# Cross-covariance attention on one core: the last unit's Q and K in 4 KB rows, the last V transfer and the last store in one piece

## The chip, the core and the metric

The kernel runs on one core of a Trainium2 chip. The metric is the device time of one execution in microseconds (us), the median of three runs: 128.64 us before the change (128.51 to 128.71). The core has a matrix engine (PE; its weight loads are listed as PEld), a vector engine (DVE), a scalar engine (ACT), a general engine (POOL) and a sync engine (SP). In this kernel SP issues almost all transfers between the chip's memory (HBM) and the on-chip memory; sixteen DMA engines carry them out.

## What is computed

Q, K and V are float32 of shape (8, 12, 512, 64): 96 heads of 512 rows by 64 columns. Attention is taken over the 64 columns, not over the 512 rows:

```
Q_norm = Q / (norm(Q, axis=-2) + 1e-10)
K_norm = K / (norm(K, axis=-2) + 1e-10)
attn = softmax(einsum('bhnd,bhne->bhde', Q_norm, K_norm), axis=-1)
out = einsum('bhnd,bhde->bhne', V, attn)
```

Each input is 12.58 MB and so is the output, so that 50.33 MB have to pass between HBM and the core.

## The kernel before

**Units.** Four heads are a unit (`HU`); there are U = 24 units, S = 12 pairs of units (unit u is half r of pair s, u = 2s + r) and W = 6 groups of four units. The last unit is u = 23, that is pair 11, half 1.

**Q and K.** `load_qk` (line 172) brings a unit of Q or of K into 128 partitions. For an ordinary unit each head fills 32 partitions with 16 rows of 64 numbers each, so that a partition receives one contiguous run of 4 KB from HBM. `WIDE` (line 118) is the first unit that is loaded differently: there a head fills 64 partitions with 8 rows each, in two halves `m`, and a partition receives two runs of 2 KB (line 183, the views `Qw` and `Kw` of lines 132 and 133). With `WIDE = U - 1` this is the last unit alone. Pairs 0 to 2 and the last pair are loaded one unit at a time, the others as whole pairs (`parts`, line 377).

**Grams.** `cast_qk` (line 209, DVE) puts Q and K of a unit side by side in bf16, and `grams` (line 221) multiplies this block by itself on PE. One product of a head gives all of Q'Q, Q'K and K'K, 128 by 128, accumulated over the steps t. An ordinary unit takes 16 steps of 4 heads, 64 matmuls over 32 partitions; the unit in 2 KB rows takes 8 steps of 4 heads, 32 matmuls over 64 partitions. Every matmul also has a weight load. From the grams the norms (`squares`, `sums`, `powers`), the scaled logits (`scale_k`, `logits`), the exponentials (`exps`) and the normalised weights `ab` (`normalise`) are made.

**V and the output.** `load_v` (line 189) brings two units' V as 128 partitions with one run of 8 KB each, a transfer of 1 MB; the last one, (w, r) = (5, 1), is brought in two halves of 4 KB runs (line 418, line 196). `cast_v` makes bf16 of it in two parts c, `vtrans` transposes on PE, `vcopy` brings the result from PSUM, `outs` multiplies by the weights, `ocopy` copies a quarter of a pair's result to the tile `so`, and `store` (line 198) writes half a pair, 512 KB, in runs of 2 KB. There are 24 such halves, i = 0 and 1 of each pair. Two are special. Store (9, 1), named `FEW` (line 122), goes out as four DMAs: 92 partitions, 4 partitions and 32 partitions of its first half, then the second half (lines 201 to 206). The last store, (11, 1), goes out as two DMAs of 256 KB in runs of 1 KB, each as soon as its own quarter is copied (lines 457 and 458).

**What sets the order.** Nothing is scheduled by the hardware: the class `Order` (line 22) simulates the engines with the costs that are written beside each piece, always takes the piece that can begin first (ties by a rank), and the program emits the pieces in that order. For DMA it assumes at most eight transfers under way (`QUEUE`, line 32), which mirrors the program: its DMAs take eight completion semaphores in turn, and a DMA is issued when the eighth before it has landed. Loads and stores are all on SP, in order. The plan also knows that PE stops now and then for more instructions: `pause` (line 44) counts PE instructions (a matmul and its weight load are two) and expects a stop at 190 and at every 256 after that, until 6.1 us after the previous one. `size` (line 353) tells it how many PE instructions a piece has: 128 for the grams of a unit, 64 for those of a unit from `WIDE` on, 16 for a transposition, 8 for half of one and for the logits, 16 for a quarter of the output.

Of the kernel before, what the change touches and what calls it, by code (L numbers as in the profile page):

```python
# [16 lines left out]
J = T // 2  # L17
# [85 lines left out]
def kernel(  # L103
# [7 lines left out]
    nc = tc.nc  # L111
    B, H, N, _ = Q.shape
    assert N == 32 * T and Q.shape[3] == D
    U = B * H // HU
    S = U // 2
    W = S // 2
    TAIL = 2
    WIDE = U - 1
    ONE = 3
    HELD, UNTIL = ("lk", 1, 1), ("cq", 0, 1)  # L120
    BOTH = S - 8
# [40 lines left out]
    qk32, v32, vb, qkb, gram, scr, kq, n2, r8, kqs, rq, lg, ex, ab, vps, vt, po, so = ({} for _ in range(18))  # L162
# [9 lines left out]
    def load_qk(s, x, r):  # L172
# [7 lines left out]
        if (s, x) == (0, 1):  # L180
            nc.scalar.dma_start(out=qk32[s][:, x, r].rearrange("p t d -> p (t d)"), in_=Ku[w, e, :, r])
        elif 2 * s + (r or 0) >= WIDE:
            nc.sync.dma_start(out=qk32[s][:, x, r].rearrange("p (m j) d -> p m (j d)", m=2), in_=(Qw, Kw)[x][U - 1])
# [11 lines left out]
        else:  # L195
            nc.sync.dma_start(out=o[:, c], in_=i[:, c])

    def store(s, i, k=None):
        rows = slice(None) if k is None else slice(k * (J // 2), (k + 1) * (J // 2))
        o = Of[s // 2, s % 2, i].rearrange("p r (j d) -> p r j d", d=D)  # L200
        if (s, i) == FEW:

            for a, b in ((0, 92), (92, 96), (96, 128)):
                nc.sync.dma_start(out=o[a:b, 0], in_=so[s, i][a:b, 0])
            nc.sync.dma_start(out=o[:, 1], in_=so[s, i][:, 1])
            return
        nc.sync.dma_start(out=o[:, :, rows], in_=so[s, i][:, :, rows])

    def cast_qk(u, x):
        s, r = divmod(u, 2)  # L210
# [10 lines left out]
    def grams(u):  # L221
# [3 lines left out]
        if r == 0:  # L225
            gram[s] = ps_g.tile([128, HU, 2, 2, 2 * D], F32, name="gram")
        for t in range(T if u < WIDE else J):
            for h in range(HU):
                if u < WIDE:
                    x = qkb[u][32 * h:32 * (h + 1), t, :]  # L230
                else:
                    x = qkb[u][64 * (h % 2):64 * (h % 2 + 1), J * (h // 2) + t, :]
                nc.tensor.matmul(gram[s][:, h, r, 0], x, x, start=(t == 0), stop=(t == (T if u < WIDE else J) - 1))  # L233

# [118 lines left out]
    def size(key):  # L353
        if key[0] == "gr" and key[1] >= WIDE:
            return 64
        return 8 if key[0] == "vt" and key[-1] is not None else {"gr": 128, "lg": 8, "vt": 16, "ou": 16}[key[0]]

    plan = Order(size)
    X = 1.29
    R = dict(cq=2.5, gr=2.471, sq=0.756, kq=1, rd=3.457, pw=3.5, sc=1, rq=1.9, lg=5, ex=1.1, nm=2.545, cv=1.165, vt=0.9, vc=1.1, ou=2, oc=0.9)  # L360
    BIAS = dict(sc=-0.6, kq=5, cv=1, vc=-0.3, oc=0.6)
    QK_PACE, V_FROM, V_PACE, ST_LAG = 0.631, 0.0377, 0.7486, 1.5133

    def v_at(v):
        return V_FROM + V_PACE * v / U

    def piece(key, engines, after, behind, rank, fn, *args):
        if key[0] in ("cv", "vc", "oc", "kq", "sc"):
            plan.add(key, engines, after, behind, rank, lambda eng: fn(eng, *args))
        else:  # L370
            plan.add(key, engines, after, behind, rank, lambda eng: fn(*args))

    def back(kind, i, n, *rest):
        return (kind, i - n, *rest) if i - n >= 0 else None
# [17 lines left out]
    for u in range(U):  # L392
        s, r = divmod(u, 2)
# [17 lines left out]
    def turns(w):  # L411
        return [(q, f) for q in range(4) for f in ((0, 1) if w == W - 1 and q >= TAIL else (None,))]

    last, turned = None, None
    for w in range(W):
        both = 2 * w >= BOTH
        for r in range(2):
            halves = (0, 1) if (w, r) == (W - 1, 1) else (None,)
            n = 2 * w + r - NB["v"]
            for c in halves:  # L420
                free = [("cv", n // 2, n % 2, h) for h in range(2)] if n >= 0 else []
                piece(("lv", w, r, c), {"DMA": X if c is not None else 2 * X}, free, [last], v_at(4 * w + 2 * r + (c or 0)), load_v, w, r, c)
                last = ("lv", w, r, c)
            for c in range(2):
                free = [("vt", w - NB["vb"], *t) for t in turns(w - NB["vb"])] if w >= NB["vb"] else []
                piece(("cv", w, r, c), {"POOL": 1.15, "DVE": (0.72, BIAS["cv"])} if both else {"POOL": 1.15},
                      [("lv", w, r, c if len(halves) == 2 else None)] + free, [("cv", w, r, 0)] if c else [], R["cv"] + 0.01 * (4 * w + 2 * r + c), cast_v, w, r, c)
        for n, (q, f) in enumerate(turns(w)):
            if f is None:
                before = turns(w)[n - 1] if n else turns(w - 1)[-1] if w else None  # L430
                wait = [("vc", w if n else w - 1, *before)] if before else []
            else:
                wait = [("kq", S - 1)] + ([("vc", w, *turns(w)[n - 4])] if n >= 4 and turns(w)[n - 4][1] is not None else [])
            piece(("vt", w, q, f), {"PE": 0.6 if f is not None else 0.8}, [("cv", w, r, c) for r in range(2) for c in range(2)] + wait, [turned],
                  R["vt"] + 0.02 * w, vtrans, w, q, f)
            turned = ("vt", w, q, f)
            copies = {"ACT": 0.74 if f is not None else 1.31}
            if both:
                copies["DVE"] = (0.74 if f is not None else 1.42, BIAS["vc"])
            free = [("ou", 2 * (w - NB["vt"]) + e, x) for e in range(2) for x in range(4)] if w >= NB["vt"] else []  # L440
            piece(("vc", w, q, f), copies, [("vt", w, q, f)] + free, [("vc", w, *turns(w)[n - 1])] if n else [], R["vc"] + 0.02 * w, vcopy, w, q, f)
    for s in range(S):
        for x in range(4):
            i, k = divmod(x, 2)
            n = 4 * s + x - 2
            wait = [("oc", n // 4, n % 4)] if n >= 0 else []
            order = [("ou", s, x - 1) if x else back("ou", s, 1, 3)]
            piece(("ou", s, x), {"PE": 0.5}, [("vc", s // 2, *t) for t in turns(s // 2) if t[0] // 2 == k] + [("nm", s)] + wait, order, R["ou"] + 0.01 * s, outs, s, x)
            n = 2 * s + i - NB["so"]
            free = [("st", n // 2, n % 2)] if k == 0 and n >= 0 else []  # L450
            order = [("oc", s, x - 1) if x else back("oc", s, 1, 3)]
            piece(("oc", s, x), {"ACT": 0.6, "DVE": (0.68, BIAS["oc"])} if s >= BOTH else {"ACT": 0.6}, [("ou", s, x)] + free, order, R["oc"] + 0.01 * s, ocopy, s, x)
        for i in range(2):
            order = [("st", s, 0) if i else back("st", s, 1, 1)]
            if (s, i) == (S - 1, 1):

                piece(("sh", s, i), {"DMA": 0.67}, [("oc", s, 2)], order, v_at(2 * s + i) + ST_LAG, store, s, i, 0)
                piece(("st", s, i), {"DMA": 0.67}, [("oc", s, 3)], [("sh", s, i)], v_at(2 * s + i) + ST_LAG, store, s, i, 1)
            else:
                piece(("st", s, i), {"DMA": X}, [("oc", s, 2 * i), ("oc", s, 2 * i + 1)], order, v_at(2 * s + i) + ST_LAG, store, s, i)  # L460

    ahead = [loaded(x, 0, r) for r in range(2) for x in range(2)]
    held, passed = [], False
# [40 lines left out]
```

## Time and profile before

| what | value |
|---|---|
| time, median of 3 runs (lowest, highest) | 128.64 us (128.51, 128.71) |
| the profiled execution: span from first to last instruction | 127.0 us |
| what lies around the span: median less span | 1.64 us |
| instructions in the profile | 4887 |
| PE matmul busy, weight loads busy | 77.7 us (61%), 62.9 us (50%) |
| DVE, ACT, POOL busy | 92.8 us (73%), 72.5 us (57%), 36.6 us (29%) |
| moved by DMA | 50.64 MB in 15629 packets, mean 399 GB/s |

The page gives the profiled execution's span but no device time of its own, so the span stands for it; the 1.64 us around it are taken as constant. The page divides the span into 40 slices of 3.2 us and shows for each the share of time that an engine was busy, in tenths, and what the DMA engines moved. Further down it lists the DMA queues, a chain of work traced back from the end, groups of like instructions with the mean duration of one, and the issues of DMAs. The trace itself can be asked for the instructions in order of time, for the busy time of each engine in a chosen stretch with the number of instructions in it, and for who waited for whom. It also holds, for each DMA, one completion event from each DMA engine that took part, and for each packet its start, duration and size.

### The profile page before, as it was taken

How to read it: one execution, taken by the hardware profiler on the slowest of the kernel's cores; microseconds unless marked ns; L12 is line 12 of the kernel's file. 1: busy time of each engine (PE TensorE's matmuls, PEld its weight loads, DVE VectorE, ACT ScalarE, POOL GpSimd, SP SyncE). 2: the span in 40 equal slices, each digit the busy share in tenths (PEclk: the TensorE clock that was granted, in tenths of full speed). 3: DMA queues.
4: the chain of work that ended last, by engine and by line, in shares of the span. 5: the costliest groups of instructions: out<-in, count | busy, mean ns of one | idle time of the engine just before them, and what ended most of it. 6: DMA issues, size and time to landing. Idle time of an engine off the chain costs nothing.

```text
span 127.0 us, 4887 instructions
## 1 busy us (share of the span) xinstructions
PE 77.7 (61%) x2128; PEld 62.9 (50%) x2128; DVE 92.8 (73%) x141; ACT 72.5 (57%) x220; POOL 36.6 (29%) x40
## 2 busy tenths in 40 slices
PE   0065384894844679858594879566797869680000
PEld 0054372773633568647482668445585748460000
DVE  3354749859899899999885898999999799820000
ACT  4000441569877077786692786794829969972000
POOL 4006307300906903033065212213453361200000
PEclk9999999999998555999958967998559995955555
DMA  4999999999999999999999999999999999999993
GB/s 114 415 434 410 430 410 418 417 437 403 425 426 415 410 419 421 405 415 426 430 410 413 415 421 427 412 419 428 401 413 410 403 402 406 401 405 408 405 366 106
DMA packets 15629, 50.64 MB, mean 399 GB/s; under 512 B 1144, under 2 KB 1656, under 8 KB 14200
## 3 DMA queue, kind: packets, MB, share of 16 engines
q1 hardware_dynamic: 15320, 49.29, 96.4%
q10 hardware_dynamic: 288, 1.05, 2.1%
q8 instruction: 16, 0.26, 0.7%
q14 instruction: 5, 0.04, 0.1%
HBM read 37.75 MB, written 12.58 MB: 396 GB/s over the span
## 4 chain that ended last, share of the span: by engine, by line
DVE 39%; DMA 21%; PE 13%; ACT 11%; issue 4%; POOL 2%; DVEq 0%; SPq 0%; POOLq 0%; ACTq 0%
DMA qk<-in_Q_dram 21%; DVE qkb L213 15%; PE gram L233 9%; DVE scr L240 7%; DVE ab L291 6%; ACT vt L166 4%; DVE vb L168 4%; ACT ex L282 3%; ACT so L166 3%; PE vps L302 3%; DVE n L252 2%; DVE vt L168 2%; DVE so L168 2%; PE po L319 1%; ACT kq L166 1%
## 5 line engine op out<-in xcount | busy, mean ns | idle before, releaser
L233 PE MATMUL gram<-qkb 32*128 32x128 bf16 (+1 forms) x1504 | 35.5, 257 | 23.1 <-DVE qkb L213 9.9
L233 PEld LDWEIGHTS <-qkb 32*128 32x128 bf16 (+1 forms) x1504 | 29.9, 114 | 27.7 <-DVE qkb L213 12.7
L213 DVE CAST qkb<-qk 128x1024 bf16<-128x1024 f32 x48 | 36.4, 780 | 8.5 <-DMA qk<-in_Q_dram 6.9
L170 POOL TENSOR_SCALAR vb<-v 128x1024 bf16<-128x1024 f32 x19 | 21.2, 1129 | 45.5 <-DMA v<-in_V_dram 32.0
L166 ACT COPY so<-po 128x512 f32<-128x512 f32 x45 | 25.0, 593 | 5.2 <-PE po L319 5.0
L166 ACT COPY vt<-vps 128x1024 bf16<-128x1024 bf16 (+1 forms) x18 | 17.8, 989 | 17.4 <-PE vps L302 17.3
L302 PE MATMUL vps<-identb,vb 128*128 128x128 bf16 x192 | 20.2, 262 | 5.8 <-POOL vb L170 3.7
L319 PE MATMUL po<-ab,vt 128*64 128x128 bf16 x384 | 19.3, 242 | 5.2 <-issue 2.7
L263 POOL TENSOR_TENSOR kqs<-kq,r 64x512 f32<-64x512 f32 x12 | 14.0, 1164 | 25.8 <-ACT r L259 13.4
L240 DVE SCALAR_TENSOR_TENSOR scr<-gram,eye 64x512 f32<-64x512 f32 x24 | 16.5, 687 | 4.4 <-PE gram L233 4.1
L302 PEld LDWEIGHTS <-vb 128*128 128x128 bf16 x192 | 14.7, 117 | 10.0 <-POOL vb L170 5.1
L319 PEld LDWEIGHTS <-vt 128*64 128x64 bf16 x384 | 13.8, 121 | 9.2 <-issue 4.6
L282 ACT ACTIVATE ex<-lg,rq 128x64 f32<-128x64 f32 x48 | 14.5, 322 | 2.8 <-PE lg L276 2.7
L166 ACT COPY kq<-gram 64x512 f32<-64x512 f32 x12 | 7.0, 581 | 13.5 <-DVE scr L240 13.4
L291 DVE TENSOR_TENSOR ab<-ex,rinv 64x256 bf16<-64x256 f32 x24 | 13.9, 579 | 0.6
L282 ACT ACTIVATION_READ_ACCUMULATOR ex<-lg,rq 128x1 f32 x48 | 10.2, 213 | 0.0
L168 DVE CAST vb<-v 128x1024 bf16<-128x1024 f32 x5 | 7.6, 1527 | 1.2 <-DMA v<-in_V_dram 1.2
L252 DVE TENSOR_REDUCE n<-scr 128x8 f32<-128x512 f32 x12 | 8.1, 679 | 0.1
L276 PE MATMUL lg<-eye,kqs 64*128 64x64 f32 x48 | 6.4, 259 | 2.6 <-issue 1.5
L168 DVE COPY vt<-vps 128x1024 bf16<-128x1024 bf16 (+1 forms) x8 | 7.9, 1019 | 0.1
L276 PEld LDWEIGHTS lg<-eye,kqs 64*128 64x128 f32 x48 | 4.5, 156 | 4.4 <-issue 2.0
L288 DVE RECIPROCAL rinv<-esum 128x4 f32<-128x4 f32 x12 | 2.1, 171 | 2.8 <-ACT ex L282 2.8
(17 smaller groups left out, 16.0 us busy)
## 6 DMA issues: line engine op xcount, KB each, us to landing
v<-in_V_dram SPq DMA_DIRECT2D x11, 1024.0 KB, 17.1
out_dram<-so SPq DMA_DIRECT2D x22, 512.0 KB, 10.2
qk<-in_Q_dram SPq DMA_DIRECT2D x8, 1024.0 KB, 17.4
qk<-in_K_dram SPq DMA_DIRECT2D x8, 1024.0 KB, 17.1
qk<-in_Q_dram SPq DMA_DIRECT2D x8, 512.0 KB, 12.2
qk<-in_K_dram SPq DMA_DIRECT2D x6, 512.0 KB, 12.5
qk<-in_K_dram ACTq DMA_DIRECT2D x2, 512.0 KB, 7.3
v<-in_V_dram SPq DMA_DIRECT2D x2, 512.0 KB
```

The source lines that it names most:

```text
L166: nc.scalar.copy(o, i)
L168: nc.vector.tensor_copy(o, i)
L170: nc.gpsimd.tensor_scalar(out=o, in0=i, scalar1=1.0, scalar2=0.0, op0=ALU.mult, op1=ALU.add)
L213: nc.vector.tensor_copy(qkb[u][:, :, x * D:(x + 1) * D], qk32[s][:, x, r])
L233: nc.tensor.matmul(gram[s][:, h, r, 0], x, x, start=(t == 0), stop=(t == (T if u < WIDE else J) - 1))
L240: nc.vector.scalar_tensor_tensor(out=scr[s][half], in0=gram[s][half, :, :, 0, half].rearrange("p h r d -> p (h r) d"), scalar=1e-20, in1=e ...
L263: (nc.vector if eng == "DVE" else nc.gpsimd).tensor_tensor(out=kqs[s][HI], in0=kq[s][HI], in1=r8[s][HI, :, None].to_broadcast([D, 2 * HU, ...
L276: nc.tensor.transpose(l[:, h, :], kqs[s][HI, 2 * h:2 * h + 2].rearrange("p r d -> p (r d)"), eye2[HI])
L282: nc.scalar.activation(e[:, h, :], lg[s][:, h, :], AF.Exp, scale=rq[s][:, h:h + 1], accum_out=z[:, h:h + 1])
L291: nc.vector.tensor_tensor(out=a[half, :, half], in0=e[half], in1=ri[half, :, None].to_broadcast([D, HU, D]), op=ALU.mult,)
L302: nc.tensor.transpose(ps[:, c, n, :], vb[w][:, J * c + j].rearrange("p r d -> p (r d)"), identb)
L319: nc.tensor.matmul(po[s, x][e * D:(e + 1) * D, j].rearrange("p r d -> p (r d)"), v, ab[s][:, h, :])
```

## The change

The constant `WIDE` becomes U, so that no unit is loaded in 2 KB rows: the last unit's Q and K come in runs of 4 KB, and its grams take 64 matmuls over 32 partitions in place of 32 over 64. They are still one transfer each for Q and K of that unit, of 512 KB. The last V transfer comes as one of 1 MB in runs of 8 KB. The last store is one of 512 KB in runs of 2 KB, and waits for both of its quarters. `size` now says 128 for the last unit's grams, and the plan is computed anew.

```diff
-    WIDE = U - 1
+    WIDE = U
...
-    def store(s, i, k=None):
-        rows = slice(None) if k is None else slice(k * (J // 2), (k + 1) * (J // 2))
+    def store(s, i):
...
-        nc.sync.dma_start(out=o[:, :, rows], in_=so[s, i][:, :, rows])
+        nc.sync.dma_start(out=o, in_=so[s, i])
...
-            halves = (0, 1) if (w, r) == (W - 1, 1) else (None,)
+            halves = (None,)
...
-            if (s, i) == (S - 1, 1):
-
-                piece(("sh", s, i), {"DMA": 0.67}, [("oc", s, 2)], order, v_at(2 * s + i) + ST_LAG, store, s, i, 0)
-                piece(("st", s, i), {"DMA": 0.67}, [("oc", s, 3)], [("sh", s, i)], v_at(2 * s + i) + ST_LAG, store, s, i, 1)
-            else:
-                piece(("st", s, i), {"DMA": X}, [("oc", s, 2 * i), ("oc", s, 2 * i + 1)], order, v_at(2 * s + i) + ST_LAG, store, s, i)
+            piece(("st", s, i), {"DMA": X}, [("oc", s, 2 * i), ("oc", s, 2 * i + 1)], order, v_at(2 * s + i) + ST_LAG, store, s, i)
```

## The prediction

> **What bounds the kernel.** I read the 40 slices first, then the DMA queues, then stretches of the end. The transfers run from the start to the end, and they outlive the computing:
>
> ```profile
> span 127.0 us, 4887 instructions
> ...
> PE   0065384894844679858594879566797869680000
> ...
> DMA  4999999999999999999999999999999999999993
> GB/s 114 415 434 410 430 410 418 417 437 403 425 426 415 410 419 421 405 415 426 430 410 413 415 421 427 412 419 428 401 413 410 403 402 406 401 405 408 405 366 106
> ...
> q1 hardware_dynamic: 15320, 49.29, 96.4%
> ...
> q8 instruction: 16, 0.26, 0.7%
> ```
>
> The DMA row has a 9 in every slice but the first and the last, PE has zeros in the last four. So the end is that of the sixteen DMA engines, and an engine's work sets it, not a wait of the computing. Keep the q8 row in mind: 16 packets of 16 KB each, which carry instructions and not data. The last copy to `so` ends at 115.07 us; SP issues stores up to 120 us:
>
> ```profile
> 114.00 1.07 ACT L166 COPY so<-po 128x512 f32<-128x512 f32 x2 [0.24 <-PE po L319]
> ...
> 115.75 4.76 SPq L207 DMA_DIRECT2D out_dram<-so  x5
> ```
>
> The five issues (the single records: 115.75, 117.05, 118.30, 119.58, 120.05) wait for a free place among the eight DMAs under way, not for data. In the stretches of the end (last two columns: DMA share, GB/s) the rate falls before it stops:
>
> ```profile
> 120.00:122.00 2.00, 0.00 (x0) 0.00 (x0) 0.00 (x0) 0.00 (x0) 0.00 (x0) 0.50 1.06 407
> 122.00:123.00 1.00, 0.00 (x0) 0.00 (x0) 0.00 (x0) 0.00 (x0) 0.00 (x0) 0.50 0.92 353
> 124.00:125.00 1.00, 0.00 (x0) 0.00 (x0) 0.00 (x0) 0.00 (x0) 0.00 (x0) 0.50 0.73 258
> 125.00:126.00 1.00, 0.00 (x0) 0.00 (x0) 0.00 (x0) 0.00 (x0) 0.00 (x0) 0.50 0.08 26
> ```
>
> The engines don't end together. The last DMA's sixteen completion events stand at 122.48, 122.69, 123.03, 124.00, 124.81, 125.07, 125.13, then eight from 125.25 to 125.54, and one alone at 126.05, which ends the execution. The store before `FEW` shows why: eight engines complete it at 116.44 to 118.09, eight at 119.11 to 119.52. Tracing the events back, each 16 KB packet makes one engine later by 1.0 to 1.5 us: the first eight packets hit eight different engines, the ninth (66.03 us) makes one of these doubly late, and by the sixteenth (108.57 us) all eight have had two. `FEW`'s 92 rows go to four of the other eight engines; one of these is now the last, 0.51 us behind the eight.
>
> **Part 1: fewer, larger packets.** In each size most packets start on their engine a fixed time after the one before: 42.3 ns at 1 KB, 80 at 2 KB, 155.4 at 4 KB, 306 at 8 KB. Per engine: Q and K of the last unit 2 x (16 x 80 - 8 x 155.4) = 74 ns; last V 16 x 155.4 - 8 x 306 = 38 ns; last store 32 x 42.3 - 16 x 80 = 74 ns; two completion packets fewer, about 10 ns. Together 0.19 us on every engine, the last one too. By the packets' own durations (46, 84, 159, 309 ns, and 9 for a completion) it is 0.36 us. I take 0.19, since starts fix the rate, and keep 0.10 and 0.36 as ends.
>
> The Trainium skill ("DMA: Bandwidth & Descriptors", "Anatomy of one DMA" and "Rules for kernel authors") gives a DMA a fixed 2.0 us and tells authors to coalesce; by that, two DMAs fewer would be worth 4 us, and the sum would be about 124.6. That formula is given for the path through the general engine; here the two halves of the last store complete 0.68 us apart on the last engine (125.37 and 126.05), half of a whole store's 1.28, so nearly all of such a cost lies under the queue.
>
> **Part 2: 64 more PE instructions.** The grams of unit 23 go from the second of these forms to the first, from 32 pairs of matmul and weight load to 64:
>
> ```profile
> L233 PE MATMUL gram<-qkb 32*128 32x128 bf16 x1472 | 34.4, 257 | 23.1 <-DVE qkb L213 9.9 <-DVE qk L179 6.7 <-issue 4.8
> ...
> L233 PE MATMUL gram<-qkb 64*128 64x128 bf16 x32 | 1.1, 217 | 0.0
> ```
>
> Their own time is cheap: 1.07 us now, 1.89 for 64 in the chain of work. What counts is the number. PE stops at intervals with nothing in the profile to wait for ("issue"):
>
> ```profile
> 62.22 0.13 PEld L276 LDWEIGHTS lg<-eye,kqs 64*128 64x128 f32 x1 [1.59 <-issue]
> ...
> 68.42 0.50 PEld L233 LDWEIGHTS <-qkb 32*128 32x128 bf16 x33 [1.59 <-issue]
> ```
>
> Cut at these stops, the number of PE and PEld instructions (x, first two pairs of columns) is:
>
> ```profile
> 0.00:62.21 62.21, 37.03 (x1119) 30.47 (x1119) 48.15 (x74) 32.65 (x96) 20.05 (x25) 0.92 0.99 404
> 62.21:68.41 6.20, 4.87 (x128) 3.95 (x128) 4.44 (x8) 4.16 (x16) 2.36 (x3) 0.72 1.00 415
> 68.41:80.80 12.39, 9.56 (x256) 7.61 (x256) 11.01 (x17) 8.52 (x22) 3.40 (x3) 0.86 1.02 417
> 86.72:104.76 18.04, 14.88 (x384) 11.80 (x384) 16.82 (x25) 13.11 (x38) 7.43 (x7) 0.81 1.03 407
> 104.76:127.00 22.24, 7.91 (x113) 6.26 (x113) 6.53 (x13) 9.45 (x32) 1.04 (x1) 0.58 0.93 356
> ```
>
> 2238 = 190 + 8 x 256, then 256, 512, and (after one of 256 not shown) 768: pages of 256 instructions, each crossing followed 3 to 6 us later by one 16 KB packet. PE resumes at 62.22, 1.3 us after the end (60.88) of the packet that the crossing before had called for, so a crossing fetches the page that begins at the next one. The last crossing is number 4030; 226 instructions follow, to 4256. The next would be 4286. With 64 more there are 4320, so it is crossed, 34 instructions before the end, and a **seventeenth packet** is due some 4 us later, near 120 us, while the engines still drain stores.
>
> Its price: it hits an engine that has had two, presumably the first of the lap, whose events have stood at the late end of the eight since (125.53). The last two packets, which fell among stores as this one will, made their engines about 1.1 us later; the packet alone lasts 0.94; the early ones, among loads, cost up to 1.5. I take 1.1. The end: 125.53 - 0.19 + 1.1 = 126.44, against 126.05 now: **+0.39 us**. From the first of the eight, 125.25, at 0.94 and a saving of 0.36 it is below the engine that is last today, and that one's saving decides; from 125.54 at 1.5 and a saving of 0.10 it is +0.89.
>
> The Trainium skill ("Runtime: NRT & Kernel Launch", "Instruction fetch mechanics") also has 256-instruction blocks of 16 KiB and calls a crossing "mostly hidden"; by that the seventeenth is free and only part 1 remains. For PE that doesn't hold in the rows above (1.59 us each), and it says nothing of the data engine that carries the packet.
>
> **Part 3: what becomes late in the computing.** Up to the grams of unit 23 PE has run 3904 instructions (1952 pairs before 99.96 us). With 128 they reach 4032, so the last pair lies beyond crossing 4030 and waits for its page. That page's packet ended at 103.37 and PE resumed at 104.77; the grams now end at 101.04. The squares of pair 11 start at 102.94 today (DVE is busy until then) and would start near 105.0, +2.1 us. V as a whole lands near 101.5, so its first cast starts 1.1 us later than at 100.36; the transpositions behind it stand behind the PE stop anyway. The last copy then ends near 117.2, or 118 if the clock, 0.5 to 1.0 in this stage, falls less well. Behind it wait the last store on SP and nothing else. SP has no place for that store before 119.58, so up to there nothing changes. Beyond that the late engines still write the store before it (completed at 123.88 to 124.20 on the eight), and a store reaches the engines about 1 us after its issue (119.58, first 1 KB packet 120.5); they lack nothing before an issue at about 122. The cover is some 5 us; were it gone, each us later would be a us.
>
> Losing the early half of the last store (part 1's other side) costs nothing either: both halves are issued after 115.07, when both have data.
>
> **Rivals.**
> *No seventeenth packet reaches the drain* (fetching ends with the program, or an early engine takes it). For: the page from 4286, which the sixteenth brought, may hold the program's last instructions; then it was needed and a further one isn't. Against: only a handful of PE instructions shows after 4256, and the sixteenth was fetched all the same. Then 126.05 - 0.19: **128.45 us**, 128.28 to 128.54: not slower.
> *The computing reaches the drain.* Decides from a last copy past 122 us, 7 us later than now; at 124 it gives 2 us more, about 130.6. Against: I count 2 to 3.
> *Fixed costs were not hidden, or the merged transfers balance the engines anew*: up to 1 us less, about 127.7. Against: other transfers in the same forms already run back to back.
>
> **The numbers.** Sums are in the profiled execution (span 127.0) and are added to the median, 128.64, 1.64 above it. The likeliest case, 0.70, gives 128.64 + 0.39 = 129.03, own range 128.45 to 129.53. No packet 0.22, computing 0.05, balance 0.03. A measurement of this kernel can tell about 0.2%, 0.26 us. Of the likeliest case 0.72 lies above that (0.50), 0.26 within (0.18), the rest below (0.02); of the second 0.35 is faster (0.08), else the same (0.14); the third is slower, the fourth faster. Faster 0.13, same 0.32, slower 0.55. Leaving out the second case would leave out too much, so the range is 128.4 to 129.5.
>
> **What would show it.** Right: q8 with 17 packets; the last PE stretch 34 instructions after a stop at 4286; a stop of about 3 us before the last pair of unit 23's grams; one late-group engine completing the last store alone, near 126.4; no packets of 1 KB. Wrong: q8 with 16; the last event again from the engine of `FEW`; copies that end past 120 us, with SP waiting for ACT at its last issue.

## The result, and the profile after

| | before | after |
|---|---|---|
| time, median (lowest, highest) | 128.57 us (128.51, 128.71) | 129.28 us (129.21, 129.49) |
| ratio, 95% interval | | 1.0049 (1.0034 to 1.0065) |
| span of the profiled execution | 127.0 us | 127.4 us |
| instructions in the profile | 4887 | 4949 |
| last completion event of the last store | 126.05 us | 126.53 us |

The changed kernel is slower by 0.6 us, 0.4 to 0.8 by the interval. The forecast was 0.39 us more, in a range that holds the measured time.

From the profile of the changed kernel, the rows that were shown of before (slices of the span, then the DMA queues: packets, MB, share of 16 engines):

```profile
span 127.4 us, 4949 instructions
...
PE   0065393994837679859475986777597729753000
...
DMA  4999999999999999999999999999999999999991
GB/s 113 413 438 408 428 411 418 417 433 408 435 418 414 411 417 424 402 415 427 423 414 414 415 428 417 415 424 425 401 420 419 401 402 410 395 408 408 375 377 60
...
q1 hardware_dynamic: 14648, 49.29, 95.9%
...
q8 instruction: 17, 0.28, 0.8%
```

The same 49.29 MB now go in 672 packets fewer on q1, and q8 has 17 packets in place of 16. PE still has its zeros at the end, but three of them in place of four. The crossing at 4030 (a crossing is the place where one block of 256 PE instructions, a page, ends and the next begins) fell into the last unit's grams, as forecast. First the weight loads of PE in order of time, then the instructions on either side of the stop (x of PE and of PEld):

```profile
99.96 0.90 PEld L232 LDWEIGHTS <-qkb 32*128 32x128 bf16 x63
104.47 0.09 PEld L232 LDWEIGHTS <-qkb 32*128 32x128 bf16 x1 [3.61 <-issue]
```

```profile
0.00:104.46 104.46, 67.98 (x2015) 55.78 (x2015) 84.43 (x127) 61.45 (x186) 36.01 (x38) 0.89 1.01 408
104.46:127.40 22.94, 9.01 (x145) 6.96 (x145) 8.48 (x16) 10.89 (x34) 1.04 (x1) 0.75 0.91 350
```

63 of the 64 pairs run, the last waits 3.61 us; 2 x 2015 = 4030 is the crossing, to the instruction. 290 instructions follow in place of 226, so that the next crossing, 4286, is passed 34 before the last. In the trace's packets the seventeenth of 16 KB starts at 117.65 us and lasts 0.96 us. What it does is seen in two places. SP in order of time:

```profile
111.44 1.93 SPq L203 DMA_DIRECT2D out_dram<-so  x3
114.30 0.37 SPq L204 DMA_DIRECT2D out_dram<-so  x1
115.63 5.50 SPq L206 DMA_DIRECT2D out_dram<-so  x4
```

The single records of the last row are 115.63, 116.91, 119.72 and 120.75: a gap of 2.8 us where 1.3 is usual, since the store eight places before was complete on fifteen engines at 118.14 and on the sixteenth at 119.65. And the end, in stretches (last two columns: DMA share, GB/s):

```profile
120.00:122.00 2.00, 0.00 (x0) 0.00 (x0) 0.00 (x0) 0.00 (x0) 0.00 (x0) 0.50 0.99 384
122.00:123.00 1.00, 0.00 (x0) 0.00 (x0) 0.00 (x0) 0.00 (x0) 0.00 (x0) 0.50 1.05 406
124.00:125.00 1.00, 0.00 (x0) 0.00 (x0) 0.00 (x0) 0.00 (x0) 0.00 (x0) 0.50 0.59 227
125.00:126.00 1.00, 0.00 (x0) 0.00 (x0) 0.00 (x0) 0.00 (x0) 0.00 (x0) 0.50 0.07 29
126.00:127.00 1.00, 0.00 (x0) 0.00 (x0) 0.00 (x0) 0.00 (x0) 0.00 (x0) 0.50 0.01 4
```

Before, the stretch from 126 on moved nothing (0 GB/s). A share of 0.07 of sixteen engines is one engine: it writes alone for about the last microsecond. The completion events of the last DMA, one from each engine, say the same:

```
before  122.48 122.69 123.03 124.00 124.81 125.07 125.13 125.25 125.28 125.31 125.34 125.37 125.41 125.53 125.54 126.05
after   123.55 123.57 123.68 124.34 124.37 124.75 125.11 125.12 125.13 125.21 125.22 125.24 125.34 125.36 125.50 126.53
```

Fifteen engines are done by 125.50 (before, by 125.54, and the sixteenth 0.5 us later). Now the sixteenth is one of the late group and is 1.0 us behind. The trace doesn't name the engine of an event; but the same lag can be followed from store to store back to the one of 118.14 and 119.65, where it sets in while the seventeenth packet is under way, so that this engine is taken to be the one that carried the packet.

### The profile page after: what moved, and what is told of

Read it like the earlier page. It is cut to its first block, busy times and chain, and to the rows that moved or that the text cites. A ratio compares the mean times of both kernels' runs of the same rounds, so it can differ in the third digit from the quotient of the medians.

```text
span 127.4 us, 4949 instructions
## 1 busy us (share of the span) xinstructions
PE 77.0 (60%) x2160; PEld 62.7 (49%) x2160; DVE 92.9 (73%) x142; ACT 72.3 (57%) x220; POOL 37.0 (29%) x39
## 3 DMA queue, kind: packets, MB, share of 16 engines
q1 hardware_dynamic: 14648, 49.29, 95.9%
## 4 chain that ended last, share of the span: by engine, by line
DVE 36%; PE 21%; DMA 19%; issue 8%; ACT 5%; SPq 1%; DVEq 0%; ACTq 0%
DVE qkb L212 15%; DMA qk<-in_K_dram 14%; PE gram L232 12%; DVE scr L239 7%; DMA qk<-in_Q_dram 5%; DVE vt L168 4%; PE vps L301 4%; DVE ab L290 4%; PE po L318 3%; ACT so L166 3%; DVE n L251 2%; ACT ex L281 2%; DVE vb L168 2%; PE lg L275 1%; SPq L185 1%
## 5 line engine op out<-in xcount | busy, mean ns | idle before, releaser
L232 PE MATMUL gram<-qkb 32*128 32x128 bf16 x1536 | 36.7, 259 | 24.8 <-issue 8.5
L232 PEld LDWEIGHTS <-qkb 32*128 32x128 bf16 x1536 | 30.8, 116 | 29.7 <-issue 11.1
L212 DVE CAST qkb<-qk 128x1024 bf16<-128x1024 f32 x48 | 37.7, 810 | 9.6 <-DMA qk<-in_Q_dram 8.0
L170 POOL TENSOR_SCALAR vb<-v 128x1024 bf16<-128x1024 f32 x18 | 21.7, 1215 | 43.9 <-DMA v<-in_V_dram 39.0
L301 PE MATMUL vps<-identb,vb 128*128 128x128 bf16 x192 | 18.5, 253 | 4.8 <-POOL vb L170 3.5
L301 PEld LDWEIGHTS <-vb 128*128 128x128 bf16 x192 | 14.0, 113 | 7.9 <-POOL vb L170 4.2
L290 DVE TENSOR_TENSOR ab<-ex,rinv 64x256 bf16<-64x256 f32 x24 | 12.8, 534 | 0.6
```

The lines of the kernel that those rows point to most:

```text
L170: nc.gpsimd.tensor_scalar(out=o, in0=i, scalar1=1.0, scalar2=0.0, op0=ALU.mult, op1=ALU.add)
L212: nc.vector.tensor_copy(qkb[u][:, :, x * D:(x + 1) * D], qk32[s][:, x, r])
L290: nc.vector.tensor_tensor(out=a[half, :, half], in0=e[half], in1=ri[half, :, None].to_broadcast([D, HU, D]), op=ALU.mult,)
L301: nc.tensor.transpose(ps[:, c, n, :], vb[w][:, J * c + j].rearrange("p r d -> p (r d)"), identb)
```

## The experiments

Three theories were held against each other. **The page:** 64 PE instructions more, past one more crossing, bring a seventeenth packet, and it makes one DMA engine the last. **The merging:** the whole V, the whole last store or the 4 KB rows fill the engines worse or come late. **The computing:** the longer grams and their stop delay the last stores. The kernel before, run beside the experiments, had 128.65 to 128.66 us; ratios are against it.

**1. Rows and grams put back**, V and store stay whole:

```diff
-    WIDE = U
+    WIDE = U - 1
```

> The changed kernel with 2 KB rows and 64-row grams put back for the last unit; V transfer and last store stay whole. Theory of the page (the seventeenth packet of PE instructions makes one twice-hit DMA engine the last): 4256 PE instructions, 16 packets, and only the saving of the merged V and store is left, 0.04 + 0.07 + 0.01 = 0.12 us: 0.1 to 0.2 us under the kernel before, about 128.45. Rival of the merging (the whole V or the whole last store is late or fills the engines worse): the loss stays, 129.0 to 129.3. Rival of the computing (longer grams and their stop delay the stores): as the theory, since the grams are short again; it is told apart by the runs with added matmuls.

128.44 us, 0.9983 (0.9975 to 0.9992), 16 packets. The loss is gone, and the merged V and store bring 0.2 us: faster than both kernels.

**2. Rows and grams alone**, the kernel before with `WIDE = U`:

> The kernel before with only the last unit's rows and grams changed (WIDE = U); V and the last store stay in halves. Theory of the page: 17 packets, the whole loss and without the 0.12 us that the merging saves: 0.1 us above the changed kernel, about 129.4 (0.8 above before). Rival of the merging: no loss, 128.5 to 128.6. Rival of the computing: as the theory, with a last copy after 115.1 us and SP waiting for ACT near the end.

129.22 us, 1.0055 (1.0042 to 1.0067), 17 packets. The whole loss is there with V and the store in halves. That it would be 0.1 us above the changed kernel doesn't show; the intervals don't separate them. With the first run this rules out a merged V or store as the cause, but the 4 KB rows and the grams still go together.

**3 to 6. Matmuls alone.** The kernel before, all its transfers as they were, with n pairs of matmul and weight load ahead of the last unit's grams, whose results the real ones overwrite; n = 14 and 16, then 8 and 24:

```diff
+        for n in range(14 if u == U - 1 else 0):
+            x = qkb[u][64 * (n % 2):64 * (n % 2 + 1), n % T, :]
+            nc.tensor.matmul(gram[s][:, n % HU, r, 0], x, x, start=True, stop=True)
         for t in range(T if u < WIDE else J):
```

> The kernel before with 14 more pairs of matmul and weight load in the last unit's grams, overwritten by the real ones; all transfers as before. 4284 PE instructions, 2 short of the crossing at 4286. Theory of the page: 16 packets, time of the kernel before within 0.1 us, 128.6. Rival of the computing: grows with the matmuls, some 0.3 us of the 0.7 (28 of the 64 instructions). Rival of the merging: no change.

> As the run with 14, but 16 more pairs: 4288 PE instructions, 2 past the crossing at 4286. Theory of the page: 17 packets and a step of the whole loss, plus 0.6 to 0.9 us over the kernel before, 129.2 to 129.5, though only four instructions more than the run with 14 pairs. Rival of the computing: within 0.05 us of the run with 14 pairs. Rival of the merging: no change against before.

These two missed: 129.15 us, 1.0040 (1.0021 to 1.0060), and 129.25 us, 1.0034 (1.0014 to 1.0055), no step between them, and both spread over more than 1.4 us (128.49 to 129.93, 128.44 to 129.86). The spans tell more. With 14 pairs all twelve are 126.7 to 127.1, as before; the time around the span (time less span of one execution), 1.74 to 1.85 in the executions of the kernel before, is 1.76 to 2.83. With 16 pairs two spans are long, 127.8 and 128.1 (the profiled one is the first, and has 17 packets), the other ten are 126.6 to 127.0 with 1.74 to 3.05 around them. So within a few instructions of the crossing it isn't the same in every execution whether the span grows, and something costs time outside the span; the traces don't show what. I had put the runs too near. The next two stand clear of it:

> The kernel before with 8 more pairs (4272 PE instructions, 14 short of the crossing at 4286), farther from it than the run with 14. Theory of the page: 16 packets in every execution, 128.66 within 0.1 us, and the time around the span at its usual 1.78 us, unlike the 1.8 to 2.8 of the run with 14 pairs. Rival of the computing: a little above before. If the spread of the run with 14 comes of the added matmuls and not of the nearness of the crossing, half of it shows here.

> The kernel before with 24 more pairs (4304 PE instructions, 18 past the crossing), farther past it than the run with 16. All transfers as before. Theory of the page: 17 packets in every execution, the spans at 127.5 to 128.1 as in the three executions of the run with 16 that had them, time 129.2 to 129.6, narrow. Rival of the computing: no more than 0.2 us over before. Rival of the merging: as before.

(The run with 16 had two such spans, not three, from 127.8 on.) With 8 pairs 128.64 us, 0.9996 (0.9987 to 1.0005): nothing. With 24 pairs 129.78 us, **1.0083 (1.0069 to 1.0097)**, all five between 129.40 and 129.93. Sixteen pairs lie between the two, at most 0.5 us of PE's time (64 take 1.89 us), and 1.1 us of the kernel's. PE doesn't stop at the crossing at 4286 in the profile (0.05 us between the instructions on either side), and the last copy ends at 116.92 us, where that of the faster seventh run, below, ends at 116.89. The queue of instructions, and the last stretches, of the run with 24 pairs:

```profile
q8 instruction: 17, 0.28, 0.8%
```

```profile
124.00:125.00 1.00, 0.00 (x0) 0.00 (x0) 0.00 (x0) 0.00 (x0) 0.00 (x0) 0.50 0.73 258
125.00:126.00 1.00, 0.00 (x0) 0.00 (x0) 0.00 (x0) 0.00 (x0) 0.00 (x0) 0.50 0.18 64
126.00:127.00 1.00, 0.00 (x0) 0.00 (x0) 0.00 (x0) 0.00 (x0) 0.00 (x0) 0.50 0.05 16
```

From 124 to 125 it moves what the kernel before moved there, 258 GB/s; then it goes on for 1 us longer, at last on one engine alone, with its event at 127.05 us, where the other fifteen are done by 126.00.

**7. All the transfers of the change, without the added instructions:**

```diff
-        for t in range(T if u < WIDE else J):
+        for t in range(J if u == U - 1 else T):
...
-                nc.tensor.matmul(gram[s][:, h, r, 0], x, x, start=(t == 0), stop=(t == (T if u < WIDE else J) - 1))
+                nc.tensor.matmul(gram[s][:, h, r, 0], x, x, start=(t == 0), stop=(t == (J if u == U - 1 else T) - 1))
```

The kernel leaves out half of the last unit's rows in its grams.

> The changed kernel, all its transfers (4 KB rows, whole V, whole store), with 8 of the 16 steps of the last unit's grams: half of that unit's rows are left out of its grams. 4256 PE instructions. Theory of the page: 16 packets, and the saving of all the merging: 0.2 us under before by the packets' spacing, 0.25 by the run with the rows put back plus 0.07, so 128.35 to 128.45. Rival of the merging (4 KB rows included): 129.0 to 129.3.

128.46 us, 0.9984 (0.9975 to 0.9993). The merging, 4 KB rows and all, isn't a loss but a gain of 0.2 us. The end, in stretches, and the queue:

```profile
q8 instruction: 16, 0.26, 0.7%
```

```profile
125.00:126.00 1.00, 0.00 (x0) 0.00 (x0) 0.00 (x0) 0.00 (x0) 0.00 (x0) 0.50 0.03 12
126.00:127.00 1.00, 0.00 (x0) 0.00 (x0) 0.00 (x0) 0.00 (x0) 0.00 (x0) 0.50 0.00 0
```

Its last copy ends at 116.89 us, later than the changed kernel's 116.62: late computing is in the faster kernel too.

**8. The engine that was last, relieved.** The first run, with store (9, 1) cut otherwise:

```diff
-            for a, b in ((0, 92), (92, 96), (96, 128)):
+            for a, b in ((0, 76), (76, 80), (80, 88), (88, 96), (96, 128)):
```

> The run with the rows put back, with the first half of store (9, 1) cut as 76, 4, 8, 8 and 32 partitions in place of 92, 4 and 32: the four engines that carry the 92 get 24 rows in place of 26, and if the pieces of 8 go to the four other early engines too, those get 4 in place of 2 and the eight late ones keep theirs. Theory that one engine's load sets the end: the engine that is last there (125.79, 0.15 us behind the late eight) ends 0.16 us earlier, level with the eight: 0.1 to 0.2 us less, 128.3. If the two more DMAs cost places among the eight under way at the end: the same or up to 0.3 us more.

128.41 us, 0.9984 (0.9976 to 0.9993), beside 128.44 of the first run. In the profiled execution the engine of `FEW` is level with the eight now (last events 125.62, 125.63, 125.66) and the last event is 0.13 us earlier, but in time that is 0.03 us, less than the runs tell apart, where 0.1 to 0.2 was expected: a miss. With the one engine relieved the eight late engines end last (125.32 to 125.66 with it), so there was little to gain.

**9. One packet fewer.** The changed kernel with five units in 2 KB rows:

```diff
-    WIDE = U
+    WIDE = U - 5
...
-            nc.sync.dma_start(out=qk32[s][:, x, r].rearrange("p (m j) d -> p m (j d)", m=2), in_=(Qw, Kw)[x][U - 1])
+            nc.sync.dma_start(out=qk32[s][:, x, r].rearrange("p (m j) d -> p m (j d)", m=2), in_=(Qw, Kw)[x][2 * s + r])
...
-        return (0, 1) if s < ONE or s == S - 1 else (None,)
+        return (0, 1) if s < ONE or s >= S - 3 else (None,)
```

> The changed kernel (whole V, whole last store) with the last five units in 2 KB rows and 64-row grams, and the last three pairs loaded unit by unit: 4000 PE instructions, 30 short of the crossing at 4030, so 15 packets, one fewer than before. Theory that one engine's load sets the end: one of the eight late engines gets only one packet and ends 1.2 us early, the other seven stay, so nothing is gained on the run with the rows put back: 128.45, up to 128.75 if 2 KB rows cost their 0.07 us a unit. Rival that each packet costs time as such, as the seventeenth did (0.8 us): 127.6 to 127.9.

129.26 us, 1.0039 (1.0027 to 1.0051), 15 packets. The rival's time did not come, but the run can't reject it by its time: it is 0.8 us above the first run and above my bound too. What speaks against the rival is the trace. Seven engines, not eight, complete the store before `FEW` late (119.62 to 120.00) and nine early (116.79 to 118.74); in the first run they are eight (119.37 to 119.69) and eight (116.59 to 118.51). One packet fewer spares one engine, as the theory has it. Eight engines end at 125.57 to 125.94, where the late eight of the first run end at 125.27 to 125.64: as much as 0.07 a unit by the packets' spacing would give for four more units in 2 KB rows (not shown: the first and the seventh run find nothing for one unit); the last engine ends 0.60 later, 126.39. SP shows that the plan came out differently:

```profile
103.36 10.47 SPq L206 DMA_DIRECT2D out_dram<-so  x6
114.87 1.11 SPq L203 DMA_DIRECT2D out_dram<-so  x3
116.02 0.48 SPq L204 DMA_DIRECT2D out_dram<-so  x1
```

Among the six are gaps of 2.6 and 3.7 us (105.91, 108.55, 112.22). By the trace SP waits there for the computing: its stores (line 206) wait six times for ACT's copies to `so`, 6.6 us in all and 3.2 at the longest, against twice and 0.9 us in the first run. Whether these, or the changed loads of two more pairs, make the rest of the 0.8 us was not tried. The time of the run says nothing on what one packet fewer is worth by itself.

**10. The cover of the computing.** The kernel before, with the last copy made nine times over:

```diff
-        copy(eng, o, po[s, x])
+        for _ in range(9 if (s, x) == (S - 1, 3) else 1):
+            copy(eng, o, po[s, x])
```

> The kernel before, with the very last copy to the output tile made nine times over, so that it ends some 8 x 0.59 = 4.7 us later, near 119.8 us. Theory that the computing is covered by some 5 us: 128.65 as before, within 0.1. Rival that the last store waits for the computing: up to 4.7 us more, or part of it.

128.70 us, 1.0005 (0.9996 to 1.0014). ACT and SP at the end, of this run:

```profile
112.64 7.46 ACT L166 COPY so<-po 128x512 f32<-128x512 f32 x12
```

```profile
115.83 4.77 SPq L207 DMA_DIRECT2D out_dram<-so  x5
```

The copies end at 120.10 us, 5.0 us later than before, and SP issues its five stores from 115.83 to 120.6 as it did (115.75 to 120.5). Five microseconds more of computing at the very end are free in this kernel: the cover is shown. It is the last store's: in the ninth run stores ahead of it did wait for copies.

## Why the prediction was right, and where it was off

**Where the end is.** Right: the DMA engines set it, and of these a single one. The tenth run shows that the computing has 5 us to spare, the eighth that relieving the one engine brings it level with the next and so gains next to nothing.

**Part 1, the packets.** 0.19 us by the packets' spacing; the seventh run measures 0.20 (0.09 to 0.32 by its interval). The shares are less sure. V and the last store alone give 0.22 in the first run, where 0.12 was worked out, and the rows, worth 0.07 on paper, add nothing that these runs could tell. The Trainium skill's formula ("DMA: Bandwidth & Descriptors", "Anatomy of one DMA"), with its fixed 2.0 us a DMA for the path through the general engine, would by estimate have given 4 us for two DMAs fewer; behind this full queue nothing like it is to be seen, only the 0.20.

**Part 2, the count.** Right in mechanism, and shown: the crossing at 4030 falls between the 63rd and the 64th pair, the one at 4286 is passed, a seventeenth packet comes (at 117.65, not near 120), and with transfers untouched it costs 1.1 us from one side of the crossing to the other. **The step that was off in size** is the packet's price, "I take 1.1". In the profile of the changed kernel one engine's event moves from at most 116.85 to 119.65 between two stores where the others of its group move by 1.27 to 1.31, which makes at least 1.5 us of delay; some of it is regained by the end, where the engine is 1.2 to 1.4 us behind the others of its group (126.53 against 125.11 to 125.36). The profiled execution has 0.48 us more at the last event, where 0.39 was forecast. The timed runs have 0.6 to 0.7, since spans of 127.4 to 127.7 stand against a median of 126.9 before, of which the profiled execution (127.0) was a late one; so the 1.64 us around the span, taken as constant, was too little for it (1.74 to 1.85 in the runs). Also, which engine of the group carries the packet isn't the same in each kernel: in the run with 24 pairs it was one of the latest (about 118.45 would have been its event, 119.93 it was), and that run lost 1.1 us; in the changed kernel it was one of the earlier, and that lost 0.8 against the seventh run; in the second run too (about 119.2, 120.61), and that lost 0.6 to 0.7 against before. I had taken the first of the lap at 125.53; in the changed kernel the others of the group end at 125.11 to 125.36, so that a base that was a little late and a price that was a little low partly made up for each other.

One bound was wrongly argued. For the first of the eight, at 0.94 and a saving of 0.36, I said that the engine which is last today decides. But 125.25 - 0.36 + 0.94 = 125.83 is later than that engine's 126.05 - 0.36 = 125.69: the packet would have decided there too, at 0.22 under before, 128.42 in place of 128.45. The range holds both.

**Part 3, the computing.** The stop is 3.61 us (about 3 was said), the squares start at 104.74 (105.0), the last copy ends at 116.62 (117.2), and none of it costs anything. What I had not counted is that SP's places depend on the slowest engine: the packet opened the gap of 2.8 us on SP, and for about a microsecond up to 120.6 three of the early engines had nothing to write (from 119.9 on 13 packets are under way in place of 16). They end early anyway, so it cost nothing here. And a store reaches the engines a little later than I read: the first 1 KB packet starts at 120.74, not 120.5, 1.2 us after its issue.

**The rivals.** No seventeenth packet: false; it was fetched though only 34 matmuls and weight loads followed, 18 in the run with 24 pairs. Late computing: false, by the seventh and the tenth run. Merged transfers worth as much as 1 us: false, they are worth 0.2.

**Open.** What happens within a few instructions of a crossing, and what it is that takes up to 1.3 us outside the span there; the traces hold no such execution. And what makes the rest of the ninth run's loss.

## What to carry to other kernels

Where the profile's end is a drain of transfers, ask which DMA engine is last and what else it carries: instruction pages travel on the same engines as the data, and one page on an engine that is already behind cost 0.6 to 1.1 us here, though all the pages together take 0.8% of the engines' time. Count PE's instructions against the page: here 8 more pairs of matmul and weight load cost nothing and 24 more cost 1.1 us. Fewer and larger transfers behind a full queue were worth about 0.2 us here, what the spacing of the packets gives, and no fixed cost for each DMA showed; and when a change holds a gain and a loss, take it apart, since here the half without the added instructions (128.44 us) beats both kernels.

## What the runs showed of the hardware that was not expected

A packet of 16 KB lasts 0.96 us, but delayed the data on its engine by at least 1.5 us at first and by 1.2 to 1.4 at the end. By the count of the crossings, pages are fetched past the last one that the matmuls need: there are 17 packets at 4304 instructions, and if each crossing calls for the page that begins at the next one, as the stops of PE suggest, the seventeenth brings what would begin at 4542. And in the runs that ended 2 instructions short of a crossing and 2 past it, the time outside the span, 1.73 to 1.90 us in all the others, rose to as much as 2.83 and 3.05.
